# A smaller DMA scratch, paired probability buffers for the last query tiles, and another place in memory for the raw operands of the gate/up stage

## The chip, the core and the metric

The kernel runs on one core of one Trainium2 chip. The metric is the device time of one execution in microseconds (us), median of the runs. PE is the matrix engine (PEld its weight load), DVE the vector engine, ACT the scalar engine, POOL the GpSimd engine, SP the engine that issues most DMAs (SPq is its queue). SBUF is the on-chip memory of 128 partitions; every address below is a byte offset within one partition, taken from the sizes of the program's tiles.

## The reference, cut to what matters

One decoder layer over 1024 positions of width 1024, in float32:

```python
h = h + rms_norm(mixer(rms_norm(h, norm_mix_pre)), norm_mix_post)
h = h + rms_norm(swiglu(rms_norm(h, norm_ffn_pre)), norm_ffn_post)
# mixer: 8 attention heads (2 groups of 4) with three softmax branches (compressed blocks,
#   selected blocks, a window of 512), mixed by gates, beside 8 chunked spatial-gating groups,
#   all through one output projection w_out
# swiglu(h) = (silu(h @ w_gate) * (h @ w_up)) @ w_down, inner width 2816
```

## The kernel before

A float32 product is made of three float32r matmuls (`mm3`, L182 to L185): each operand is split into a rounded part (`hi`, a cast on ACT, L167) and a remainder (`lo`, a subtraction on DVE or POOL, L173), and hi*hi, hi*lo and lo*hi are summed in PSUM.

The stages follow each other: norm and input projections, compressed keys and values, attention, gate/up, down projection. A planner orders the instructions of each engine before the run by times of its own; each engine then works its list strictly in that order. `tc.high_priority(n)` moves a block ahead in the planner's choice, otherwise program order decides between instructions that are ready.

**Memory.** Tiles live in pools, and pools are stacked from two ends. The left stack begins behind the DMA scratch (16,384 bytes, at address 0) and grows up; the right one begins at 229,344 and grows down. When a pool is closed its bytes are handed to the next pool opened there, and a new tile waits until every tile that held any of its bytes has been read for the last time (`reuse_waits="tile"`). So the stack order decides what a load or a split has to wait for.

**Attention** (L639 to L762) goes over the eight query tiles of 128 rows from tile 7 down to tile 0, and in each over four pairs of heads (`g`, `pr`). For each head, PE makes logits in a PSUM bank `a` (L673, L674; two banks, handed out strictly in turn), DVE adds the bias and writes them to the head's probability buffer `L` with its running minimum (L678, L682), ACT takes exponentials in place (L721), POOL multiplies by gate over sum in place (L732), PE transposes the blocks (L745), ACT and DVE split them (`ph`, `pl`), and PE multiplies with the values `vt` and `vch` (L752, L754). There are six `L` buffers of 6,912 bytes, taken in turn; tiles 7 to 0 use 64 heads in all. The queries of a pair are loaded by `load_q` (L567) two pairs ahead and split on POOL. In pair 1 of a tile `output_proj` of the tile before is issued (L595, matmuls into banks `w`), in pair 3 its `pre_ffn` (L625), which writes the normalised, transposed rows to DRAM (`h2_scr[1]` for tiles 7 to 4, `h2_scr[0]` for tiles 3 to 0, L637). For tile 0 both come behind the loop (L763).

**Gate/up** is one level of a Strassen-like scheme with seven products. Seven regions of 16,384 bytes on the right hold the activation operands (`bps`, L783). `raw1` is half 1 of the rows (loaded from `h2_scr[1]`, L802), `b12` and `b22` are its split halves; `praw` is the raw weights of the first column block (L813), `pop` and four `op` tiles their splits. `plain_pass(1, b12, b22)` (L874) is the first matmul work of the stage, 96 matmuls of 512 columns, and needs nothing of tiles 3 to 0. Then `raw0` is loaded (half 0, needs tile 0's `h2_scr` rows), split to `b11`, `b21`, `plain_pass(0, ...)` runs, and sums and splits of `raw0` and `raw1` give `t1` to `t4`. Only then is `raw0`'s memory handed to the sums `s` of the weights (L939), which the products 6, 7, 5 and 3 of the next block need; the products 1, 2 and 4 do not.

The addresses that matter, before:

| region | address | region | address |
|---|---|---|---|
| L0 .. L5 | 126,464 .. 167,936 | r1t4 (`raw1`, later `t4`) | 212,480 .. 228,864 |
| o, q (queries) | 167,936 .. 179,712 | b22 | 196,096 .. 212,480 |
| bias tables B, C, MW | 181,248 .. 194,560 | b12t3 (`b12`, later `t3`) | 179,712 .. 196,096 |
| `vt` | 194,560 .. 210,944 | t1 (`pop`, later `t1`) | 163,328 .. 179,712 |
| `kt0`, `kt1` (keys) | 210,944 .. 227,840 | t2 | 146,944 .. 163,328 |
| `vch` | 227,840 .. 228,864 | b11 (`praw`, later `b11`) | 130,560 .. 146,944 |

Of the kernel before, what the change touches and what calls it, by code (L numbers as in the profile page):

```python
# [9 lines left out]
F32 = mybir.dt.float32  # L10
F32R = mybir.dt.float32r
# [6 lines left out]
P = 128  # L18
S = 1024
# [51 lines left out]
def trunk_kernel(ctx, tc, x, rel_bias, norm_mix_pre, norm_mix_post, norm_ffn_pre, norm_ffn_post, w_in,  # L71
# [3 lines left out]
    nc = tc.nc  # L75
# [37 lines left out]
    def turn(key, tags):  # L113
        n = turns.get(key, 0)
        turns[key] = n + 1
        return bank(tags[n % len(tags)])
# [435 lines left out]
    at = {}  # L552
    for nm in ("pt", "mix", "late", "L", "o", "q"):
        if nm == "L":
            at[nm] = Ring("at_L", 6, "left")
            at[nm].pools.reverse()
            g_at.append(at[nm])
            continue
        g_, at[nm] = pool("at_" + nm, 1, "left")
        g_at.append(g_)  # L560
# [6 lines left out]
    def load_q(i, g, pr):  # L567
        qr = at["q"].tile([P, 2, P], F32, name="qr", bufs=2)
        h0 = g * R + 2 * pr
        for dup in range(2):  # L570
            nc.sync.dma_start(out=qr[64 * dup:64 * dup + 64],
                              in_=q_scr[h0:h0 + 2, :, i * P:(i + 1) * P].rearrange("h d t -> d h t"))
        qt = at["q"].tile([P, 2, 2, P], F32R, name="qt", bufs=4)
        split(qt[:, 0], qt[:, 1], qr, "pool", "pool")
        return qt
# [3 lines left out]
    qts = {}  # L579
    for key in order[:2]:  # L580
        qts[key] = load_q(*key)
# [7 lines left out]
    HP0, HP, HP2, HO, HF, HQ, HS, HV = 400, 100, 150, 100, 400, 300, 600, 200  # L589
# [48 lines left out]

    for ti, i in enumerate(TILES):  # L639
# [5 lines left out]
        for g in range(G):  # L645
            for pr in range(2):
# [15 lines left out]
                with tc.high_priority(HP0 if at_ < 4 else HP if i >= 4 else HP2):  # L662
                    for hh in range(2):
                        r = pr * 2 + hh
                        h = g * R + r
                        L = at["L"].tile([P, 64 + S + 640], F32, "L")
# [96 lines left out]
    pre_ffn(TILES[-1], *output_proj(TILES[-1]))  # L763
# [10 lines left out]
    def acc_bank():  # L774
        if fbanks is None:
            return turn("plain", "awap")
        return fbanks.tile([P, 512], F32, name="fb")
# [5 lines left out]
    for tag in ("r1t4", "b22", "b12t3", "t1", "t2", "b11", "b21"):  # L783
        g_, bps[tag] = pool("ffn_" + tag, 1, "right")
        g_b.append(g_)

    def btile(tag, dtype=F32R):
        return bps[tag].tile([P, 2, HK, 512], dtype, name="b_" + tag, tag=tag)
# [9 lines left out]
    def h2_load(dst, half):  # L798
        for a in range(2):
            for kq in range(2):  # L800
                k = a * HK + 2 * kq
                nc.sync.dma_start(out=dst[:, a, 2 * kq:2 * kq + 2], in_=h2_scr[half][:, k:k + 2, :])  # L802

    raw1 = btile("r1t4", F32)
    h2_load(raw1, 1)
# [5 lines left out]
    def load_w(r, m, fp, a):  # L811
        c0 = m * DFF + fp * 256
        nc.sync.dma_start(out=r, in_=wgu[:, a * HK:(a + 1) * HK, c0:c0 + 256])  # L813
# [47 lines left out]
    pop = bps["t1"].tile([P, 4, 2, HK, P], F32R, name="plain_op", tag="t1")  # L861
    plain = {}
    for m in range(2):
        for a in range(2):
            load_w(praw[:, m, a], m, 0, a)
    for j in range(2):
        for m in range(2):
            plain[m, j] = [operand(praw[:, m, a, :, j * P:(j + 1) * P], pop[:, 2 * m + a] if j == 0 else None)
                           for a in range(2)]
    for a, dst in enumerate((b12, b22)):  # L870
        for k in range(HK):
            bsplit(dst, raw1[:, a, k], k)
# [39 lines left out]
    t1 = btile("t1")  # L912
    for k in range(HK):
        bsplit(t1, raw0[:, 0, k], k, PF_T1)
# [4 lines left out]
    t4_ = btile("r1t4")  # L919
# [287 lines left out]
```

## Time and profile before

| what | value |
|---|---|
| median of 3 runs | 1248.43 us (1248.29 to 1248.55) |
| the profiled execution | 1249.3 us, of which the span of instructions is 1247.6 us |
| PE busy | 1204.6 us (97%) |
| DVE, ACT, POOL busy | 917.0, 569.7, 379.5 us |
| mean granted clock of PE | 0.994 |

The busy time is summed over stages with different limits, so a stage is read from its own stretch of the timeline: which engine is idle there, and what ended its wait. [...]

### The profile page before, as it was taken

How to read it: one execution, taken by the hardware profiler on the slowest of the kernel's cores; microseconds unless marked ns; L12 is line 12 of the kernel's file. 1: busy time of each engine (PE TensorE's matmuls, PEld its weight loads, DVE VectorE, ACT ScalarE, POOL GpSimd, SP SyncE). 2: the span in 40 equal slices, each digit the busy share in tenths (PEclk: the TensorE clock that was granted, in tenths of full speed). 3: DMA queues.
4: the chain of work that ended last, by engine and by line, in shares of the span. 5: the costliest groups of instructions: out<-in, count | busy, mean ns of one | idle time of the engine just before them, and what ended most of it. 6: DMA issues, size and time to landing. Idle time of an engine off the chain costs nothing. (4 is left out here: it accounts for less than half of the span.)

```text
span 1247.6 us, 18252 instructions
## 1 busy us (share of the span) xinstructions
PE 1204.6 (97%) x6074; PEld 1006.7 (81%) x6074; DVE 917.0 (74%) x2075; ACT 569.7 (46%) x1266; POOL 379.5 (30%) x453
## 2 busy tenths in 40 slices
PE   6999999889999999999899999999999999999997
PEld 5888878868888888887687888888888888888886
DVE  5646247658898899876589877877787647588996
ACT  4423022247777778876544332333332324544452
POOL 3315112164444455642151222201222201132341
PEclk9999999999999999999899999999999999999999
DMA  7213453331111222215604233223233189333335
GB/s 255 85 68 87 133 185 116 106 100 46 43 48 47 61 64 71 66 56 159 226 37 145 96 122 127 94 91 107 89 127 126 53 281 365 120 110 85 93 119 202
DMA packets 106229, 143.86 MB, mean 115 GB/s; under 512 B 8120, under 2 KB 64792, under 8 KB 106136
## 3 DMA queue, kind: packets, MB, share of 16 engines
q1 hardware_dynamic: 99552, 133.43, 32.7%
q10 hardware_dynamic: 4280, 5.08, 1.2%
q0 software_dynamic: 2304, 4.20, 1.2%
q8 instruction: 48, 0.79, 0.3%
q14 instruction: 45, 0.37, 0.1%
HBM read 103.60 MB, written 40.71 MB: 116 GB/s over the span
## 5 line engine op out<-in xcount | busy, mean ns | idle before, releaser
L960 DVE TENSOR_TENSOR cc<-fb,cc 128x512 f32<-128x512 f32 x140 | 94.3, 687 | 56.8 <-PE fb L185 55.9
L732 POOL TENSOR_SCALAR L<-L,wts 128x64 f32<-128x64 f32 (+8 forms) x192 | 107.1, 580 | 88.3 <-DVE wts L727 56.6
L721 ACT ACTIVATE L<-L,mm 128x64 f32<-128x64 f32 (+8 forms) x192 | 116.2, 607 | 23.8 <-DVE mm L678 23.0
L849 POOL TENSOR_TENSOR cc<-sil 128x512 f32<-128x512 f32 x22 | 35.2, 1601 | 288.0 <-issue 225.5
L173 DVE TENSOR_TENSOR pl<-ps_t,ph 128x512 fp32r<-128x512 f32 (+2 forms) x168 | 102.9, 619 | 20.9 <-ACT ph L167 20.4
L167 ACT CAST ph<-ps_t 128x512 fp32r<-128x512 f32 (+2 forms) x168 | 87.1, 531 | 43.7 <-PE ps_t L745 39.2
L167 ACT CAST op<-s 128x512 fp32r<-128x512 f32 x80 | 49.4, 620 | 121.1 <-PE fb L185 107.2
L184 PE MATMUL fb<-wdo,hido 128*128 128x512 f32 x264 | 102.7, 389 | 0.0
L183 PE MATMUL fb<-wdo,hido 128*128 128x512 f32 x264 | 101.9, 389 | 0.0
L185 PE MATMUL fb<-wdo,hido 128*128 128x512 f32 x264 | 100.4, 389 | 0.0
L184 PE MATMUL fb<-b_b,op 128*128 128x512 f32 x256 | 99.6, 389 | 0.0
L185 PE MATMUL fb<-b_b,op 128*128 128x512 f32 x256 | 99.4, 389 | 0.0
L183 PE MATMUL fb<-b_b,op 128*128 128x512 f32 x256 | 99.3, 389 | 0.0
L745 PE MATMUL ps_t<-ident,L 128*128 128x128 f32 (+1 forms) x592 | 93.9, 274 | 3.6 <-POOL L L732 2.6
L173 DVE TENSOR_TENSOR hido<-hidr,hido 128x512 fp32r<-128x512 f32 x77 | 60.8, 801 | 26.7 <-ACT hido L167 26.6
L673 PE MATMUL ps_a<-kt,qt 128*128 128x448 f32 (+4 forms) x208 | 75.0, 364 | 4.7 <-DVE L L682 2.0
L745 PEld LDWEIGHTS ps_t<-ident,L 128*128 128x128 f32 (+1 forms) x592 | 68.2, 137 | 12.4 <-POOL L L732 4.6
L167 ACT CAST hido<-hidr 128x512 fp32r<-128x512 f32 x77 | 47.3, 619 | 65.8 <-PE fb L185 26.7
L1039 POOL TENSOR_TENSOR tt<-wdr 128x512 f32<-128x512 f32 x22 | 36.1, 1644 | 134.7 <-DVE wdo L173 79.9
L167 ACT CAST op<-wraw 128x512 fp32r<-128x512 f32 x60 | 37.0, 622 | 84.6 <-PE fb L185 73.1
L173 DVE TENSOR_TENSOR op<-s,op 128x512 fp32r<-128x512 f32 x80 | 63.7, 801 | 15.1 <-ACT op L167 14.2
L752 PE MATMUL ps_p<-ph,vt 128*128 128x256 f32 x264 | 73.3, 295 | 0.2 <-ACT ph L167 0.2
(357 smaller groups left out, 3458.5 us busy)
## 6 DMA issues: line engine op xcount, KB each, us to landing
wraw<-in_w_gate_up_dram SPq DMA_DIRECT2D x40, 512.0 KB, 3.5
hidr<-hid_scr SPq DMA_DIRECT2D x77, 256.0 KB, 2.7
hid_scr<-sil SPq DMA_DIRECT2D x44, 256.0 KB, 2.0
wdr<-in_w_down_dram SPq DMA_DIRECT2D x44, 256.0 KB, 5.3
hid_scr<-cc SPq DMA_DIRECT2D x33, 256.0 KB, 2.0
xt<-in_x_dram SPq DMA_DIRECT2D x16, 512.0 KB, 4.9
raw<-in_w_in_dram SPq DMA_DIRECT2D x16, 512.0 KB, 3.5
gm_scr<-gmt SPq DMA_DIRECT2D x16, 256.0 KB, 2.7
```

The costliest lines, as they stand in the source:

```text
L167: nc.scalar.copy(hi, src)
L173: e.tensor_tensor(lo, src, fl(hi), op=ALU.subtract)
L183: nc.tensor.matmul(ps, sh, mh, start=first, stop=False)
L184: nc.tensor.matmul(ps, sh, ml, start=False, stop=False)
L185: nc.tensor.matmul(ps, sl, mh, start=False, stop=last)
L673: nc.tensor.matmul(ps[:, :w], qt[:, 0, hh, :], kt_[g][:, c0:c0 + w], start=True, stop=False)
L721: nc.scalar.activation(L[:, c0:c1], L[:, c0:c1], AF.Exp, bias=mm[:, col:col + 1], scale=-1.0, accum_out=sums[:, hh, br:br + 1])
L732: nc.gpsimd.tensor_scalar(pts[hh][:, c0:c1], pts[hh][:, c0:c1], wts[:, hh, br:br + 1], 1.0, op0=ALU.mult, op1=ALU.mult)
L745: nc.tensor.transpose(ps[:kk, (bi * 2 + hh) * P:(bi * 2 + hh + 1) * P], pts[hh][:, c0:c0 + kk], ident)
L752: nc.tensor.matmul(pv[:, :256], v, ph[:kk, bi * 256:(bi + 1) * 256], start=(gi == 0 and bi == 0), stop=False)
L960: nc.vector.tensor_tensor(dst, ps, y_, op=ALU.add)
L1039: eng.tensor_tensor(dst, x_, y_, op=op)
```

## The change

Five parts:

1. The DMA scratch at the bottom of SBUF shrinks from 16,384 to 2,048 bytes. The whole left stack moves down by 14,336 bytes; the right one stays.
2. The attention pools are stacked in the order pt, mix, late, o, q, L, so that the six L buffers lie on top. Tiles 7 to 4 use six of them, tile 3 uses five (L0 to L4), and tiles 2 to 0 use L0 to L2, each holding both heads of a pair. The first two pairs' queries are loaded into L5 and split into L4.
3. On the right, `raw1` shares a region with `t1` instead of `t4`, and `pop` with `t4` instead of `t1`; the order of the regions changes.
4. `output_proj` and `pre_ffn` of tile 0 get priority (HE = 100), loads and splits of the first gate/up operands are interleaved in another order, `t3` is split before `t1`.
5. The accumulators of the two plain passes come from banks a, a, a, p instead of a, w, a, p (only the first pass uses them).

The addresses after, from the same sizes:

| region | address | region | address |
|---|---|---|---|
| o, q | 112,128 .. 123,904 | t4 (`pop`, later `t4`) | 212,480 .. 228,864 |
| L0, L1, L2 | 123,904 .. 144,640 | b22 | 196,096 .. 212,480 |
| L3, L4 | 144,640 .. 158,464 | b12t3 | 179,712 .. 196,096 |
| L5 | 158,464 .. 165,376 | r1t1 (`raw1`, later `t1`) | 163,328 .. 179,712 |
| nothing | 165,376 .. 181,248 | b11 (`praw`, later `b11`) | 146,944 .. 163,328 |
| `vt`, keys, `vch`, bias tables | as before | t2 | 130,560 .. 146,944 |

```diff
-    for nm in ("pt", "mix", "late", "L", "o", "q"):
+    for nm in ("pt", "mix", "late", "o", "q", "L"):
         if nm == "L":
             at[nm] = Ring("at_L", 6, "left")
-            at[nm].pools.reverse()
...
-    for key in order[:2]:
-        qts[key] = load_q(*key)
+    q0r = at["L"].pools[5][1].tile([P, 2, 2, P], F32, name="L")
+    q0t = at["L"].pools[4][1].tile([P, 2, 2, 2, P], F32R, name="L")
+    for n, key in enumerate(order[:2]):
+        qts[key] = load_q(*key, (q0r[:, n], q0t[:, n]))
...
+    def lring(i):
+        n = lturn["n"]
+        lturn["n"] += 1
+        ps_ = at["L"].pools
+        if n < 4:
+            return ps_[3 - n][1]
+        return ps_[5 - (n - 4) % 6][1] if i > 3 else ps_[4 - n % 5][1]
+
+    def lpair(n):
+        return at["L"].pools[2 - n % 3][1]
...
+                    if i <= 2:
+                        Lp = lpair(at_).tile([P, 2, 832], F32, name="L")
...
-                        L = at["L"].tile([P, 64 + S + 640], F32, "L")
+                        L = Lp[:, hh] if i <= 2 else lring(i).tile([P, 64 + S + 640], F32, name="L")
...
-    pre_ffn(TILES[-1], *output_proj(TILES[-1]))
+    with tc.high_priority(HE):
+        pre_ffn(TILES[-1], *output_proj(TILES[-1]))
...
-            return turn("plain", "awap")
+            return turn("plain", "aaap")
...
-    for tag in ("r1t4", "b22", "b12t3", "t1", "t2", "b11", "b21"):
+    for tag in ("t4", "b22", "b12t3", "r1t1", "b11", "t2", "b21"):
...
-    raw1 = btile("r1t4", F32)
-    h2_load(raw1, 1)
+    raw1 = btile("r1t1", F32)
...
-    pop = bps["t1"].tile([P, 4, 2, HK, P], F32R, name="plain_op", tag="t1")
+    pop = bps["t4"].tile([P, 4, 2, HK, P], F32R, name="plain_op", tag="t4")
...
-    for m in range(2):
-        for a in range(2):
-            load_w(praw[:, m, a], m, 0, a)
-    for j in range(2):
-        for m in range(2):
-            plain[m, j] = [operand(praw[:, m, a, :, j * P:(j + 1) * P], pop[:, 2 * m + a] if j == 0 else None)
-                           for a in range(2)]
-    for a, dst in enumerate((b12, b22)):
-        for k in range(HK):
-            bsplit(dst, raw1[:, a, k], k)
+    for a in range(2):
+        h2_load(raw1, 1, a)
+        load_w(praw[:, 0, a], 0, 0, a)
+    for a in range(2):
+        load_w(praw[:, 1, a], 1, 0, a)
+    for a, dst in enumerate((b12, b22)):
+        plain_op(0, 0, a)
+        for k in range(HK):
+            bsplit(dst, raw1[:, a, k], k)
+    for a in range(2):
+        plain_op(1, 0, a)
+    for m in range(2):
+        for a in range(2):
+            plain_op(m, 1, a)
...
-    t1 = btile("t1")
-    for k in range(HK):
-        bsplit(t1, raw0[:, 0, k], k, PF_T1)
...
     sub_all(raw0[:, 1], raw0[:, 1], raw1[:, 1])
-    t4_ = btile("r1t4")
+    t1 = btile("r1t1")
+    for k in range(HK):
+        bsplit(t1, raw0[:, 0, k], k, PF_T1)
+    t4_ = btile("t4")
...
-    nc = _bacc.Bacc("TRN2", target_bir_lowering=False, num_devices=1)
+    nc = _bacc.Bacc("TRN2", target_bir_lowering=False, num_devices=1, dynamic_dma_scratch_size=2048)
```

## Rows read from the trace of the kernel before

**Rows 1.** The page: busy time of PE, and the queue of POOL's DMAs.
```profile
PE 1204.6 (97%) x6074; PEld 1006.7 (81%) x6074; DVE 917.0 (74%) x2075; ACT 569.7 (46%) x1266; POOL 379.5 (30%) x453
...
q0 software_dynamic: 2304, 4.20, 1.2%
```

**Rows 2.** Windows: length, busy us of five engines, clock, DMA share, GB/s.
```profile
400.00:500.00 100.00, 98.53 (x644) 85.50 (x643) 89.60 (x349) 77.48 (x208) 48.61 (x85) 1.00 0.22 65
500.00:550.00 50.00, 47.86 (x307) 40.70 (x305) 41.80 (x186) 42.03 (x137) 30.59 (x64) 1.00 0.20 61
...
594.00:604.00 10.00, 5.45 (x13) 4.26 (x14) 7.68 (x14) 8.93 (x19) 0.55 (x1) 0.66 0.91 342
...
650.00:660.00 10.00, 7.64 (x31) 5.10 (x30) 8.53 (x7) 2.93 (x6) 8.03 (x6) 1.00 0.41 131
660.00:1200.00 540.00, 540.00 (x2384) 447.27 (x2383) 411.21 (x583) 200.60 (x349) 105.99 (x66) 1.00 0.39 130
```

**Rows 3.** Timeline of PE, 590 to 604: start, length, ..., [idle before <-releaser].
```profile
590.46 0.28 PE L754 MATMUL ps_p<-pl,vt 128*128 128x256 f32 x1
592.19 0.50 PE L183 MATMUL ps_w<-whi,mixh 128*128 128x512 f32 x1 [1.46 <-ACT mixh L167]
...
593.23 0.62 PE L185 MATMUL ps_w<-whi,mixl 128*128 128x512 f32 x2
598.55 0.80 PE L183 MATMUL ps_a<-b_b12t,plain_op 128*128 128x512 f32 x1 [4.71 <-ACT b_b12t L167]
...
603.83 0.40 PE L183 MATMUL ps_a<-b_b12t,plain_op 128*128 128x512 f32 x1
```

**Rows 4.** Timeline of SP's DMA queue, 588 to 597.
```profile
588.75 0.53 SPq L813 DMA_DIRECT2D plain_raw<-in_w_gate_up_dram  x1
589.37 2.59 SPq L802 DMA_DIRECT2D b_r1t<-h_scr  x4
592.15 4.85 SPq L813 DMA_DIRECT2D plain_raw<-in_w_gate_up_dram  x3
```

**Rows 5.** Timeline of ACT and DVE, 595 to 606.
```profile
595.05 0.62 ACT L167 CAST plain_op<-plain_raw 128x512 fp32r<-128x512 f32 x1 [2.91 <-DMA plain_raw<-in_w_gate_up_dram]
...
597.89 1.13 ACT L167 CAST b_b12t<-b_r1t 128x512 fp32r<-128x512 f32 x2
...
603.48 2.49 DVE L173 TENSOR_TENSOR b_b<-b_r1t,b_b 128x512 fp32r<-128x512 f32 x4
```

**Rows 6.** Timeline of ACT, 620 to 624: the first casts of raw0.
```profile
620.81 2.33 ACT L167 CAST b_b<-raw 128x512 fp32r<-128x512 f32 x4 [1.22 <-DMA raw<-h_scr]
```

**Rows 7.** Timeline of POOL and DVE, 634 to 652: splits, first weight sum.
```profile
634.33 6.34 POOL L173 TENSOR_TENSOR b_b12t<-b_r1t,b_b12t 128x512 fp32r<-128x512 f32 x2 [24.28 <-ACT b_b12t L167]
...
648.85 2.56 POOL L173 TENSOR_TENSOR b_r1t<-raw,b_r1t 128x512 fp32r<-128x512 f32 x2 [1.83 <-issue]
...
651.43 0.69 DVE L939 TENSOR_TENSOR s<-wraw 128x512 f32<-128x512 f32 x1 [1.83 <-POOL b_r1t L173]
```

**Rows 8.** Timeline of DVE, PE and POOL at two changes of query tile.
```profile
453.30 0.22 DVE L678 CUSTOM_DVE_ANT_0 L<-ps_a,C 128x64 f32<-128x64 f32 x1
...
461.92 0.60 PE L745 MATMUL ps_t<-ident,L 128*128 128x128 f32 x4
...
489.56 0.22 DVE L678 CUSTOM_DVE_ANT_0 L<-ps_a,C 128x64 f32<-128x64 f32 x1
...
491.69 3.27 POOL L732 TENSOR_SCALAR L<-L,wts 128x64 f32<-128x64 f32 x6 [2.77 <-DVE wts L727]
```

**Rows 9.** Timeline of PE and POOL where attention begins.
```profile
240.83 0.28 PE L185 MATMUL ps_p<-w2s,chidT 128*128 128x64 f32 x1
...
242.59 0.40 POOL L171 TENSOR_SCALAR qt<-qr 128x256 fp32r<-128x256 f32 x1 [7.82 <-DMA qr<-q_scr]
```

**Rows 10.** The tile gmh: the DMAs that POOL issues.
```profile
L601 POOL DMA_DIRECT2D gmh<-gm_scr x16: 535/574/777, 250.5 to 560.7; - x16
...
DMA to landing us min/median/max: 2.8/3.1/4.4
```

More of the change, by code (lines that the diff above doesn't have):

```diff
@@ L565, in load_bc, with load_q @@
         bcast_load(bc["post"], norm_mix_post[0])
-    def load_q(i, g, pr):
-        qr = at["q"].tile([P, 2, P], F32, name="qr", bufs=2)
+    def load_q(i, g, pr, start=None):
+        if start is None:
+            qr = at["q"].tile([P, 2, P], F32, name="qr", bufs=2)
+            qt = at["q"].tile([P, 2, 2, P], F32R, name="qt", bufs=4)
+        else:
+            qr, qt = start
         h0 = g * R + 2 * pr
@@ L572, in load_q @@
                               in_=q_scr[h0:h0 + 2, :, i * P:(i + 1) * P].rearrange("h d t -> d h t"))
-        qt = at["q"].tile([P, 2, 2, P], F32R, name="qt", bufs=4)
         split(qt[:, 0], qt[:, 1], qr, "pool", "pool")
@@ L588, in trunk_kernel @@
     wout_args = {}
-    HP0, HP, HP2, HO, HF, HQ, HS, HV = 400, 100, 150, 100, 400, 300, 600, 200
+    HE, HP0, HP, HP2, HO, HF, HQ, HS, HV = 100, 400, 100, 150, 100, 400, 300, 600, 200
     PVB, OPB, OB = "p", "w", 1
@@ L637, in pre_ffn @@
             nc.sync.dma_start(out=h2_scr[i // 4][:, 4 * b:4 * b + 4, (i % 4) * P:(i % 4 + 1) * P], in_=tl)
+    lturn = {"n": 0}
+    def lring(i):
[7 more added lines that the diff above has]
+        return at["L"].pools[2 - n % 3][1]
     for ti, i in enumerate(TILES):
@@ L796, in bsplit, with h2_load @@
         split(dst[:, 0, k], dst[:, 1, k], src, "act", "dve" if k < pool_from else "pool")
-    def h2_load(dst, half):
-        for a in range(2):
+    def h2_load(dst, half, *parts):
+        for a in parts or range(2):
             for kq in range(2):
@@ L860, in trunk_kernel, with plain_op @@
     praw = bps["b11"].tile([P, 2, 2, HK, 256], F32, name="plain_raw", tag="b11")
-    pop = bps["t1"].tile([P, 4, 2, HK, P], F32R, name="plain_op", tag="t1")
+    pop = bps["t4"].tile([P, 4, 2, HK, P], F32R, name="plain_op", tag="t4")
     plain = {}
+    def plain_op(m, j, a):
+        plain.setdefault((m, j), [None, None])[a] = operand(praw[:, m, a, :, j * P:(j + 1) * P],
+                                                            pop[:, 2 * m + a] if j == 0 else None)
+    for a in range(2):
[9 more added lines that the diff above has]
+        plain_op(1, 0, a)
     for m in range(2):
         for a in range(2):
-            load_w(praw[:, m, a], m, 0, a)
-    for j in range(2):
-        for m in range(2):
-            plain[m, j] = [operand(praw[:, m, a, :, j * P:(j + 1) * P], pop[:, 2 * m + a] if j == 0 else None)
-                           for a in range(2)]
-    for a, dst in enumerate((b12, b22)):
-        for k in range(HK):
-            bsplit(dst, raw1[:, a, k], k)
+            plain_op(m, 1, a)
     def plain_pass(half, blo, bhi):
```

## The prediction

> **What bounds the kernel now.** I read the page first, then the windows stage by stage, then the timelines of the stretches where PE is idle. PE is busy for 97% of the span [rows 1], and from 660 to 1200 us it never stops: 2384 matmuls in 540 us, 0.2265 us each [rows 2]. No part of the change lies there, so it can only win or lose in the other stretches, and the largest loss near it is the seam between attention and gate/up. The timeline of PE shows the seam. The last product with the values starts at 590.46; then PE waits 1.46 us for tile 0's last mixing operand, ends tile 0's output projection at 593.85 (593.23 + 0.62), and waits again, 4.71 us, until 598.55, when the first gate/up matmul starts [rows 3]. [...] A second, smaller stop follows at 650 to 660, where PE is busy for 7.64 of 10 us [rows 2].
>
> What ends the 4.71 us is a cast of `b12`, and that cast waits for data. SP issues the load of `raw1` at 589.37 and most of the raw weights from 592.15 [rows 4]; the DMA engines are 0.91 busy from 594 to 604 [rows 2]; the first split of the weights starts at 595.05 behind a wait for its load, that of `b12` at 597.89 [rows 5]. Both loads were late because of where they lie: `raw1` over the keys and `vch`, which the very last pair still reads, and `praw` over L0 to L2.
>
> **Part by part.** *The raw loads.* After the change `raw1` (163,328 up) shares bytes only with L5, and `praw` (146,944 up) with L3 to L5. Tile 3 is the last to use L3 and L4, tile 4 the last with L5, so both loads can go out from the start of tile 2 at about 490 [rows 8], a hundred microseconds early. The 4 MB are hidden under tiles 2 to 0, where the DMA share is 0.20 [rows 2]; without that cover they would cost what they cost now. What is late next? `pop` lies on the keys and `vch`, `b12` and `b22` on the bias tables, `vt` and a key: all wait for the last values product at 590.46 or shortly before it. So the splits start at about 591. Sixteen of them are needed for the first pass, at DVE's pace of 0.62 us (four in 2.49 us) [rows 5], while each k-step of PE takes 3 x 0.2265 = 0.68 us. PE can go from tile 0's projection (593.85) straight into gate/up instead of at 598.55: 4.7 us less. I leave the 1.46 us before as they are; a gain of all of it is the bound. If PE does not stand long, the twelve slow matmuls run at 0.2265: 12 x (0.44 - 0.2265) = 2.6 us less. Against that, DVE also has tile 0's norm and residual between the splits, some five 512-wide operations, 5 x 0.62 = 3.1 us, with priority HE. PE can use up the splits made before them, so I charge half, +1.5 us; the bounds are 0 and 4.5 us (all of it, and half of the clock loss again).
>
> *`raw0` and tile 0's chain.* The second pass needs `raw0`, cast from 620.81 [rows 6]. The first pass is 96 matmuls, 96 x 0.2265 = 21.7 us; from 593.85 with 1.5 us of holes it ends at 617.1. Today's first split of `raw0` would be whole at 620.81 + 0.62 (cast) + 0.62 (remainder) = 622.0, which is 4.9 us too late. The chain before it is tile 0's norm, residual, second norm, transposes, a write and a read of DRAM, and it shares DVE and ACT with the sixteen splits (16 x 0.62 = 9.9 us of DVE). HE moves exactly this chain ahead of them, so I take it as early enough: 0, bound +4.9 us.
>
> *`t1`, `t4` and the weight sums.* Before, `t4` waited for `raw1`'s memory, its POOL splits ended at 651.41 (648.85 + 2.56), and only then the first sum started, at 651.43 [rows 7]; PE lost 10 - 7.64 = 2.36 us [rows 2]. After, `t4` waits for `pop`, which the second pass ends with, and `t1` for `raw1`; products 1, 2 and 4 (3 x 12 x 0.2265 = 8.2 us) still cover the sums, and DVE's work there starts earlier with `raw0`. I take 1.5 us of the 2.36, bounds 0 and 2.36. POOL's splits took 3.17 us each when DVE ran beside them and 1.28 when it hardly did [rows 7]. [...]
>
> *Buffers of tiles 3 to 0.* The depth is the same or nearly so (three pairs; five heads in tile 3), but the turns collide. The last head of tile 4 is number 31 and lies in L2 (5 - 27 % 6), and the first of tile 3, number 32, in L2 too (4 - 32 % 5). The first pair of tile 2 (number 20) takes L0, the buffer of tile 3's last head (39). Each first pair thus waits until the pair before it is transposed. Now head 32 is written from 453.30, while head 31's transposes run until about 462 (one group of four starts at 461.92); tile 2's first head is written from 489.56, while POOL scales tile 3's last pair from 491.69 to 494.96 [rows 8]. So two first pairs start 7 to 9 us later. Behind them stand all later logits, since the two banks `a` are handed out in turn. PE has other work: the output projection of the tile before, 48 matmuls or 10.9 us, and DVE is 90% and 84% busy around there [rows 2], so it catches up. I charge 1.5 us in all; bounds 0 and 10 us.
>
> *Entry to attention.* The first queries now land in L5, over the compression's `chidT` (159,360 up), last read at 240.83; before, POOL split them at 242.59 [rows 9]. A load after 241.1 comes at best 1 us later, with value projections to fill PE. +0.5 us, bounds -1.5 and +2. *Banks a, a, a, p, the order of loads, the scratch itself:* 0. Banks `w` are still tile 0's, so no wait is lost or added before two accumulators are full; POOL issues 16 small DMAs of 0.57 us in the whole kernel, two for each tile [rows 10].
>
> The sum: -4.7 - 2.6 + 1.5 + 0 - 1.5 + 1.5 + 0.5 = -5.3 us. The profiled execution took 1249.3 us, so 1244.0; it is 0.9 above the median of the runs, which becomes 1248.4 - 5.3 = 1243.1.
>
> **Rivals.** *Tile 0's chain is the new bound.* If `raw0` comes when it comes now, PE stands 4.9 us after the first pass: 1248.0, no change. For it: DVE and ACT still have all the splits to do beside it. Against: HE, and 9.9 us of splits that it may pass. 0.12.
> *The splits are the new bound.* The first splits can't start before 591, and if PE stands for 4.5 us while they are made, the seam is only moved: -5.3 + 3.0, and without the gain at 650 to 660, 1246.9; no change. For it: `b12` and `b22` still wait for `vt`. Against: 0.62 is below 0.68. 0.08.
> *The colliding turns make it slower.* At each of the two tile changes PE runs dry for half of the 9 to 11 us of delay, 10 us together: -5.3 - 1.5 + 10 = +3.2, 1251.6. It decides from 6.8 us. For it: PE has 0.98 of 1 in 400 to 500 and no spare pair. Against: the projections wait there as filler. 0.12.
> *The small scratch stalls POOL.* If the second of two DMAs had to wait for the first, POOL's scaling behind it would be 3.1 us late (the median landing) in each of eight tiles [rows 10]; if half of that reached PE, -5.3 + 12.4 = +7.1 us, 1255.5. Against: 2304 packets in all [rows 1], for 16 DMAs on 16 engines 9 each, and two such DMAs a tile. [...] 0.04.
>
> **How the numbers follow.** The forecast has 0.64. What a measurement here tells from no change is about 0.2%, 2.5 us. Faster by more: the forecast, 0.64. Within: the first two rivals, 0.20. Slower: the last two, 0.16. The bounds of the terms reach down to 1238 (all of 1.46 and 2.36, no charge at the tile changes); upward I take the slower rival's edge, 1251, which leaves about 0.2 outside.
>
> **What would show it.** `raw1` and `praw` issued before 560; the first gate/up matmul within 1 us of tile 0's projection, at full clock; no wait of PE for a cast of `b_b` at the second pass; PE's idle time in 650 to 660 below 1 us. The turns show as late writes to L at the two tile changes and idle PE near 465 and 500. I am wrong if attention ends several us later, or if a wait for splits as long as 4.7 us stands in place of the old one.

## The result, and the profile after

The kernel after takes 1265.12 us (median of 4, 1264.83 to 1267.01) against 1248.49 of before on the same chip: 16.6 us slower, ratio 1.0129 (95% interval 1.0106 to 1.0151). Forecast were 1243.1 us and, at the upper end of the range, 1251. Its profiled execution took 1265.1 us with a span of 1263.4.

The windows of the kernel after, with the columns of [rows 2]:

```profile
400.00:500.00 100.00, 96.45 (x615) 81.88 (x614) 83.25 (x315) 74.05 (x193) 47.43 (x80) 1.00 0.17 54
500.00:550.00 50.00, 47.80 (x295) 39.39 (x294) 44.10 (x188) 39.94 (x128) 30.06 (x59) 1.00 0.52 167
...
650.00:660.00 10.00, 10.00 (x46) 8.29 (x45) 8.26 (x11) 4.43 (x8) 10.00 (x4) 1.00 0.07 26
660.00:1200.00 540.00, 537.63 (x2371) 444.51 (x2371) 407.26 (x570) 196.60 (x341) 115.50 (x73) 1.00 0.38 130
```

PE issues 615 matmuls from 400 to 500 us where it issued 644, and 295 against 307 in the 50 us behind: attention is already late there. The stop of PE at 650 to 660 [rows 2] has only moved on, beyond 660: PE is idle for 2.37 us there (540 - 537.63) against 2.36 before. The seam, in the timeline of PE after:

```profile
603.08 0.28 PE L773 MATMUL ps_p<-pl,vt 128*128 128x256 f32 x1
604.39 0.73 PE L183 MATMUL ps_a<-b_b12t,plain_op 128*128 128x512 f32 x2 [1.03 <-ACT b_b12t L167]
606.37 0.80 PE L184 MATMUL ps_a<-b_b12t,plain_op 128*128 128x512 f32 x1 [1.24 <-DVE b_b12t L173]
...
611.66 0.50 PE L184 MATMUL ps_a<-b_b12t,plain_op 128*128 128x512 f32 x1
...
614.31 0.39 PE L183 MATMUL ps_w<-whi,mixh 128*128 128x512 f32 x1
...
615.44 0.62 PE L185 MATMUL ps_w<-whi,mixl 128*128 128x512 f32 x2
...
637.64 1.22 PE L183 MATMUL fb<-b_b,plain_op 128*128 128x512 f32 x2 [4.83 <-ACT b_b L167]
```

Against [rows 3] the reader sees three things. The last product with the values comes 12.6 us later. The first gate/up matmul follows it after 1.31 us instead of 8.09: this is what the change was forecast to win. Not all of it is won, because 1.66 us of the 8.09 were the last six matmuls of tile 0's output projection [rows 3, 592.19 to 593.85], which have only moved behind; PE's idle time at the seam falls from 6.17 us (1.46 + 4.71) to 2.27 us (1.03 + 1.24). And that projection, which ended ahead of gate/up before, now ends inside it, at 616, and some 22 us later PE's wait of 4.83 us for the first cast of `raw0` ends, a wait that was not there before. What stood in ACT's and DVE's queues ahead of the operand that the projection needed (timeline of ACT and DVE after):

```profile
601.04 2.18 ACT L167 CAST plain_op<-plain_raw 128x512 fp32r<-128x512 f32 x4
603.45 0.37 ACT L775 COPY otmp<-ps_p 64x256 f32<-64x256 f32 x1 [0.24 <-PE ps_p L773]
603.73 2.18 ACT L167 CAST b_b12t<-b_r1t 128x512 fp32r<-128x512 f32 x4
605.81 2.17 ACT L167 CAST b_b<-b_r1t 128x512 fp32r<-128x512 f32 x4
607.89 0.29 ACT L167 CAST mixh<-os 128x128 fp32r<-128x128 f32 x1
...
602.61 2.48 DVE L173 TENSOR_TENSOR plain_op<-plain_raw,plain_op 128x512 fp32r<-128x512 f32 x4
605.01 0.58 DVE L778 TENSOR_TENSOR os<-ps_p,otmp 64x128 f32<-64x128 f32 x2
610.45 0.28 DVE L173 TENSOR_TENSOR mixl<-os,mixh 128x128 fp32r<-128x128 f32 x1
```

`mixh` and `mixl` stand last, behind eight casts and eight remainders of `b12` and `b22`. PE's own list has the projection late as well: its six matmuls start at 614.31, behind 25 gate/up matmuls and 3.6 us after `mixl` is ready (610.73). Everything that follows from them is late, to the first cast of `raw0`:

```profile
636.97 2.39 ACT L167 CAST b_b<-raw 128x512 fp32r<-128x512 f32 x4 [6.25 <-DMA raw<-h_scr]
```

16.2 us later than [rows 6]. The raw loads themselves went out as forecast, 77 to 90 us before they did (DMA queue of SP, after):

```profile
502.01 2.04 SPq L832 DMA_DIRECT2D plain_raw<-in_w_gate_up_dram  x4
...
512.22 2.76 SPq L822 DMA_DIRECT2D b_r1t<-h_scr  x4
```

The change from tile 3 to tile 2, timeline of POOL and DVE after: POOL scales tile 3's last pair, DVE then writes tile 2's first head, POOL scales that pair.

```profile
501.61 3.39 POOL L751 TENSOR_SCALAR L<-L,wts 128x64 f32<-128x64 f32 x6 [1.52 <-ACT mixh L167]
...
510.05 0.22 DVE L697 CUSTOM_DVE_ANT_0 L<-ps_a,C 128x64 f32<-128x64 f32 x1 [0.87 <-PE ps_t L764]
...
516.48 2.84 POOL L751 TENSOR_SCALAR L<-L,wts 128x64 f32<-128x64 f32 x6 [2.38 <-DVE wts L746]
```

From one scaling to the next it takes 14.87 us; DVE's write is released by a transposition of the pair before, which by the rule of the turns reads the same buffer, L0. Before, the write came 2.1 us ahead of the last pair's scaling [rows 8].

The entry to attention, timeline of SP's queue and POOL, in the kernel before:

```profile
259.87 0.81 SPq L130 DMA_DIRECT2D wo_raw<-in_w_out_dram  x2
...
264.73 1.05 POOL L161 TENSOR_SCALAR whi<-wo_raw 128x1024 fp32r<-128x1024 f32 x1 [3.34 <-DMA wo_raw<-in_w_out_dram]
...
268.21 4.34 POOL L732 TENSOR_SCALAR L<-L,wts 128x64 f32<-128x64 f32 x6
```

The same with PE, after:

```profile
249.93 11.68 SPq L574 DMA_DIRECT2D qr<-q_scr  x12
261.65 12.39 SPq L130 DMA_DIRECT2D wo_raw<-in_w_out_dram  x3
...
270.22 1.04 POOL L161 TENSOR_SCALAR whi<-wo_raw 128x1024 fp32r<-128x1024 f32 x1 [8.98 <-DMA wo_raw<-in_w_out_dram]
...
273.67 4.34 POOL L751 TENSOR_SCALAR L<-L,wts 128x64 f32<-128x64 f32 x6
...
274.04 0.71 PE L764 MATMUL ps_t<-ident,L 128*64 128x128 f32 x2 [6.13 <-POOL L L751]
```

In both kernels POOL has the split of the first output weight queued ahead of the first pair's scaling. Before, PE waits 2.0 us for that scaling; after, the weight comes 5.5 us later (270.22 against 264.73) and PE waits 6.13 us. The loads of output weights leave SP's queue, behind twelve loads of queries, only 1.8 us later than before (261.65 against 259.87); the larger part is their way from issue to landing, 8.4 to 9.0 us against 4.8 to 6.2.

The first microseconds differ too. Timeline of SP's queue and of ACT's, first in the kernel before, then after:

```profile
4.86 5.38 SPq L130 DMA_DIRECT2D xt<-in_x_dram  x2
...
167.19 0.32 ACTq L415 DMA_DIRECT2D pos_nat<-in_cmp_pos_k_dram  x1
```

```profile
0.80 0.42 ACTq L415 DMA_DIRECT2D pos_nat<-in_cmp_pos_k_dram  x1
...
7.01 3.30 SPq L130 DMA_DIRECT2D xt<-in_x_dram  x2
```

Four small loads of the compression, which went out at 167 to 173 us, now go out at 0.8 to 6.3 us, and the second pair of loads of x leaves SP 2.15 us later.

**A table of lateness.** The profiled executions reach attention between 0.4 us earlier and 3.4 us later than that of before, so the runs below are compared from one event on: POOL's fill of the bias table (L508), at 233.89 us before and 235.01 after. The table gives starts, in us later (+) or earlier than in the kernel before; all columns but the first are counted from that fill. "First pair" is the sum (L778) of tile 7's first pair, "tile 3" and "tile 2" that of their last pairs, "last PV" the last product with the values, "raw0" its first cast, "967" the matmul of the main loop that stood at 967.0 us before, "end" the last matmul. Each row is one execution: the profiled one took 2.5 us more than its kernel's median in e1 and 3.1 more in e11, 2.7 less in e7 and 2.1 less in e10, so a difference below some 3 us at the end of two rows is not an effect by itself.

| run | fill | first pair | tile 3 | tile 2 | last PV | first gate/up | raw0 | 967 | end |
|---|---|---|---|---|---|---|---|---|---|
| after | +1.1 | +4.3 | +3.0 | +9.8 | +11.5 | +4.7 | +15.0 | +14.7 | +14.7 |
| e1_turns | +3.4 | +5.1 | +3.7 | +4.2 | +5.9 | -0.9 | +9.6 | +9.2 | +9.2 |
| e2_entry | +0.5 | -1.4 | -1.8 | +5.3 | +6.8 | +0.4 | +10.4 | +10.9 | +10.9 |
| e3_chain | +2.4 | +4.6 | +3.3 | +10.1 | +12.0 | +5.4 | +8.7 | +7.5 | +7.5 |
| e4_scratch | +2.6 | +0.1 | -0.7 | -1.1 | +0.4 | -2.3 | +1.5 | +0.8 | +0.8 |
| e5_three | +0.6 | -1.6 | -2.0 | +1.3 | +3.2 | -3.4 | +1.3 | +0.7 | +0.7 |
| e6_pool | +0.5 | -1.2 | -1.6 | +1.7 | +3.5 | -3.3 | +2.3 | +0.4 | +0.4 |
| e7_swap | +0.9 | -2.6 | -3.3 | 0.0 | +2.0 | -4.6 | -1.3 | -2.5 | -2.6 |
| e8_late | +1.1 | -1.3 | -1.7 | +1.6 | +2.4 | +6.0 | +3.2 | +6.8 | +14.1 |
| e9_anchor | +0.2 | -2.2 | -4.4 | -4.6 | -2.7 | -8.6 | -2.9 | -4.7 | -4.8 |
| e10_hold | +0.3 | -2.5 | -4.7 | -4.9 | -4.1 | -10.8 | -2.9 | -3.5 | -3.5 |
| e11_scratch_anchor | +0.4 | +0.1 | 0.0 | 0.0 | 0.0 | -0.2 | +0.1 | +2.9 | +2.9 |
| e12_torder | +0.3 | -1.2 | -3.4 | -3.6 | -2.8 | -9.5 | -0.8 | -1.4 | +6.4 |
| e13_after_anchor | -0.4 | +4.8 | +3.6 | +10.4 | +12.1 | +5.3 | +15.4 | +15.0 | +15.0 |
| e14_late2 | +0.6 | -2.1 | -4.3 | -4.5 | -3.7 | +0.2 | -2.4 | +1.1 | +8.4 |

The row of after holds the story: 4.3 us lost at the entry, 6.8 between the ends of tiles 3 and 2, 6.8 won at the seam (+11.5 to +4.7, with the 1.66 us of projection that only moved), 10.3 lost again up to `raw0`.

### The profile page after: what moved, and what is told of

It is laid out like the page before. It is cut to its first block, busy times and chain, and to the rows that moved or that the text cites. A ratio compares the mean times of both kernels' runs of the same rounds, so it can differ in the third digit from the quotient of the medians.

```text
span 1263.4 us, 18216 instructions
## 1 busy us (share of the span) xinstructions
PE 1209.8 (96%) x6074; PEld 1007.8 (80%) x6074; DVE 917.4 (73%) x2075; ACT 569.4 (45%) x1266; POOL 384.9 (30%) x453
## 5 line engine op out<-in xcount | busy, mean ns | idle before, releaser
L751 POOL TENSOR_SCALAR L<-L,wts 128x64 f32<-128x64 f32 (+8 forms) x192 | 109.7, 593 | 83.5 <-DVE wts L746 46.9
L773 PE MATMUL ps_p<-pl,vt 128*128 128x256 f32 x264 | 72.8, 299 | 1.6 <-DVE pl L173 1.5
```

What stands on the lines that cost most here:

```text
L751: nc.gpsimd.tensor_scalar(pts[hh][:, c0:c1], pts[hh][:, c0:c1], wts[:, hh, br:br + 1], 1.0, op0=ALU.mult, op1=ALU.mult)
L773: nc.tensor.matmul(pv[:, :256], v, pl[:kk, bi * 256:(bi + 1) * 256], start=False, stop=last)
```

## Experiments

**e1_turns: the buffers of L in an order without collision.**

```diff
-        return ps_[5 - (n - 4) % 6][1] if i > 3 else ps_[4 - n % 5][1]
+        return ps_[5 - (n - 4) % 6][1] if i > 3 else ps_[(33 - n) % 5][1]
 ...
-        return at["L"].pools[2 - n % 3][1]
+        return at["L"].pools[2 - (n + 1) % 3][1]
```

> The kernel after, with the turns of L ordered so that each tile change takes the buffer that was freed longest ago: tile 3's heads start at L1 instead of L2, tile 2's pairs at L2 instead of L0. Theory A (four separate delays; the colliding turns are one): in the kernel after the pairs run 4.1 us late at the end of tile 3 and 10.9 us late at the end of tile 2; the 6.8 us between them are the collision, so the time falls by about 7 us, 1258, and the first head of tile 2 is written within 2 us of the last of tile 3. Theory B (the early raw loads delay the tile change: the DMA engines are 0.95 busy from 510 to 520 us): the turns matter little, the lateness of 10 us after tile 2 stays, 1264 to 1266.

1259.55 us, ratio 1.0082 (1.0061 to 1.0102). In the table the loss between tiles 3 and 2 falls from 6.8 to 0.5 us, the end from +14.7 to +9.2. POOL's scalings at this tile change:

```profile
503.34 3.29 POOL L751 TENSOR_SCALAR L<-L,wts 128x64 f32<-128x64 f32 x6 [4.71 <-DVE wts L746]
...
511.17 2.86 POOL L751 TENSOR_SCALAR L<-L,wts 128x64 f32<-128x64 f32 x6 [3.35 <-DVE wts L746]
```

7.83 us apart instead of 14.87 (7.69 in the kernel before), with the early raw loads still under this stretch. The collision cost 5.5 us by the table, 5.6 by the medians; theory B (the early loads' traffic) falls.

**e2_entry: the first two loads of output weights on ACT's queue.**

```diff
+    def wload(src, raw=None, leng=None, q=None):
 ...
-        dma(view(raw), src)
+        (q or nc.sync).dma_start(out=view(raw), in_=src)
 ...
-            wo[k] = wload(w_out_v[:, k, :], raw, WOE)
+            wo[k] = wload(w_out_v[:, k, :], raw, WOE, nc.scalar if len(wo) < 7 else None)
```

> The kernel after, with the first two loads of the output weights on ACT's queue instead of SP's, where they stand behind twelve loads of queries. Theory A: the lateness of the first pair (5.4 us, of which 4 to 5 us never come back) is the wait for these weights on POOL, which scales the first pair only after it has split them; the time falls by 4 to 5 us, 1260.5, and PE's longest wait for POOL's scaling near 275 us falls from 6.1 to about 2 us. Theory B: the first logits, 1.7 us late because the queries of the first pairs lie over the last tiles of the compression, are the delay that stays: the gain is 3 us at most, 1262 to 1265.

1261.81 us, ratio 1.0095 (1.0076 to 1.0115); the first pair comes at -1.4 instead of +4.3, the end at +10.9: 3.8 us. The planner now also places the first scaling ahead of the weights' split on POOL, and it orders the whole of attention anew:

```profile
261.58 0.90 ACTq L158 DMA_DIRECT2D wo_raw<-in_w_out_dram  x2
...
265.93 4.37 POOL L751 TENSOR_SCALAR L<-L,wts 128x64 f32<-128x64 f32 x6 [5.01 <-DVE wts L746]
270.27 2.06 POOL L161 TENSOR_SCALAR whi<-wo_raw 128x1024 fp32r<-128x1024 f32 x2
```

PE's longest wait for POOL's scaling in that stretch, 6.1 us in after, is 0.3 here. Theory A in what POOL waits for, but not in the reason that it gave: on ACT's queue the loads leave at the same time as on SP's (261.58 against 261.65), and POOL's first split starts at the same time (270.27 against 270.22). The place on SP's queue cost next to nothing; what the edit took away is the place of the weights' split ahead of the scaling in POOL's list. By the medians it gives 3.3 us.

**e3_chain: the last mixing operand of the last pair on POOL.**

```diff
-                    split(mixh[:, g * 2 + pr, :], mixl[:, g * 2 + pr, :], os_)
+                    me = ("pool", "pool") if at_ == len(order) - 1 else ("act", "dve")
+                    split(mixh[:, g * 2 + pr, :], mixl[:, g * 2 + pr, :], os_, *me)
```

> The kernel after, with the last mixing operand of the last pair split on POOL, which is idle there, instead of on ACT and DVE behind sixteen splits of the gate/up stage. Theory A: tile 0's chain is late only by that place in the queues; the projection ends some 6 us earlier, the first cast of raw0 comes at about 631 instead of 637, PE's 4.8 us of waiting before the second pass and the slow clock behind it go: 6 to 8 us less, 1258. Theory B: the norm and the transposes of the chain still share DVE and ACT with the splits, and the load of raw0 comes as late as before: 1263 to 1265.

1258.07 us, ratio 1.0065 (1.0044 to 1.0086). POOL has the operand ready at 608.9, the first cast of `raw0` comes at 631.87:

```profile
607.22 0.79 POOL L171 TENSOR_SCALAR mixh<-os 128x128 fp32r<-128x128 f32 x1 [11.36 <-DVE os L778]
608.09 0.77 POOL L173 TENSOR_TENSOR mixl<-os,mixh 128x128 fp32r<-128x128 f32 x1
...
631.87 2.38 ACT L167 CAST b_b<-raw 128x512 fp32r<-128x512 f32 x4 [1.80 <-DMA raw<-h_scr]
```

The wait of 4.83 us is gone, while e1 and e2, which leave this split alone, still have it (4.94 and 4.8 us). The end moves from +14.7 to +7.5: 7.2 us (7.1 by the medians), theory A. With the operand on POOL the planner also puts the projection's first matmul third among those of gate/up, so the run shows the worth of both places together.

**e4_scratch: before, with `dynamic_dma_scratch_size=2048` alone.**

> The kernel before, with nothing but the dynamic DMA scratch of 2 KB. Theory A: the scratch alone changes nothing, 1248.4 within 0.2%, and the queue of POOL's DMAs looks as in the kernel before (median landing 3.1 us). Theory B (the small scratch makes the second of two DMAs wait for the first): POOL's scaling behind it is late by some 3 us in each tile, 1251 to 1256, and it is part of the 16.6 us.

1250.84 us, ratio 1.0009 (0.9999 to 1.0019); the queue of POOL's DMAs has a median landing of 3.1 us as before. The rival "the small scratch stalls POOL" falls. What the scratch does change are addresses: all tiles of the left stack lie 14 KB lower, the four small loads no longer wait for memory, and they go out at 0.8 to 6.1 us here too. The planner's order of attention is another one as well.

**e5_three: the edits of e1, e2 and e3 together.**

> The kernel after with all three edits: turns, weights on ACT's queue, last operand on POOL. Theory A (three separate delays that add up): counted from the last fill of the bias tables, the kernel after ends 14.7 us later than the kernel before; the three runs of one edit each took 5.5, 3.8 and 7.2 us off; all three give 14.7 - 16.5 = 1.8 us earlier than before: 1245.5 to 1248. Theory B (they overlap: what one gives back, another wait takes): at least 4 us more than that, 1251 or above.

1250.62 us, ratio 1.0018 (1.0006 to 1.0030): some 14 us of the 16.6 are accounted for by three places, but it takes 2.6 to 5 us more than theory A gave, just short of theory B. By the table 3.3 us are lost between the ends of tiles 3 and 2 (-2.0 to +1.3), where e1 with the same turns lost 0.5, and the seam is entered later than the edits promised: the last product with the values is at +3.2 though tile 2 ended at +1.3.

**e6_pool and e7_swap: two more edits on e5.** e6 puts the remainders of the second half of the plain weights on POOL (`leng="pool"` for j = 1). e7 swaps `q0r` and `q0t` between L5 and L4.

> As e5, and the remainders of the second half of the plain weights on POOL instead of DVE. Theory A: these splits, made ready early by the early loads, stand on DVE ahead of the last pair's remainders; without them the last product with the values comes 1 us earlier, and DVE has 2.5 us less to do in the seam: 1 to 2 us less than e5. Theory B (POOL and DVE hold each other up, and the last operand waits behind them on POOL): 0 to 3 us more than e5.

1251.16 us, 1.0018 (1.0009 to 1.0027): no difference from e5; theory A's gain of 1 to 2 us is not there.

> As e5, and the first two pairs' raw queries in L4, over a tile that is free earlier, with their split in L5. The order of instructions on all engines is that of e5. Theory A (the entry's loss was the wait for the output weights): the first logits come 1 to 2 us earlier, and the time is that of e5 within 1 us, because value projections fill PE there. Theory B (the entry is paced by the first queries): 1.5 us or more less than e5.

1250.41 us, 1.0016 (1.0004 to 1.0027): no difference that its runs show, though the first pair of its profiled execution is 1.0 us earlier. Theory A, the entry is not paced by the first queries.

**e8_late: e5 with the placement undone.**

```diff
-    for tag in ("t4", "b22", "b12t3", "r1t1", "b11", "t2", "b21"):
+    for tag in ("t4", "r1t1", "b12t3", "b22", "t2", "b11", "b21"):
```

> As e5, with the raw operands placed on memory that is read to the end of attention again (raw1 on the bias tables' side, the plain weights over L1 to L3), so that their loads can't go early: the placement of the change taken back by itself. Theory A: the early loads are worth what the seam shows, some 5 us (the first gate/up matmul 1.3 us behind the last product with the values, against 8.1 before): 1251 to 1254. Theory B (the early loads give back what they win, since their splits crowd the last pair): within 2 us of e5.

1263.61 us, ratio 1.0123 (1.0107 to 1.0139), 13 us over e5. PE waits at the seam as it did before, and longer:

```profile
605.63 1.22 PE L183 MATMUL ps_a<-b_b12t,plain_op 128*128 128x512 f32 x2 [8.24 <-ACT b_b12t L167]
```

The table splits the 13 us: 6.1 up to 967 us (+0.7 to +6.8), and 7.3 behind it, in the down projection, where PE has waits of 2.3, 1.4 and 1.1 us that e5 has not. So neither theory's number holds for the whole; where the 7.3 us come from is read below, behind e14.

**e9_anchor and e11_scratch_anchor: the four small loads held back.** e9 is e7 with this, e11 is e4 with it.

```diff
+        nc.vector.tensor_copy(pn[:, 0:1], state["qs"][0:16, 0:1])
         nc.scalar.dma_start(out=pn, in_=pos[0]...
 ...
+        nc.vector.tensor_copy(w2r[:, 0, 0:1], state["qs"][:, 0:1])
         nc.scalar.dma_start(out=w2r, in_=w2[0]...
```

> As e7 (three edits and the swapped queries), and the four small loads of the compression (positions and second weights) made to wait for the last queries, by a copy of one column of theirs into each destination. Theory A: with the 2 KB scratch all tiles lie 14 KB lower, these four loads no longer wait for memory, go out at 0.8 to 6 us instead of at 167 to 173, and slow the first loads; all nine programs with the small scratch reach the fill of the bias tables 0.5 to 3.4 us later than the kernel before. Held back, the first eight loads on SP's queue go out as in the kernel before (the last pair of them at 4.9 instead of 7.0 us), and the time falls by 1 to 2 us against e7: 1248 to 1249. Theory B (the first 20 us differ by chance from run to run): no change, 1250.4.

1244.12 us, ratio 0.9963 (0.9950 to 0.9976): faster than both kernels. The loads of x leave SP at 4.90 us again, and the fill comes at +0.2. But 6.3 us against e7 are more than the start can give. The two profiled executions (1247.70 and 1244.75 us) show 2.95 of them: 0.7 at the fill, and 2.2 behind it, where tile 2 ends 4.6 us earlier than in e7: the 3.3 us that e5 and e7 lose between the ends of tiles 3 and 2 are not lost here (-4.4 to -4.6). Behind the held loads the planner makes another order of the whole attention; that this order is what wins them was not tested by itself.

> The kernel before with the 2 KB scratch (as e4) and the same four loads held back. Theory A (addresses are all that the scratch changes): the 0.1% that e4 was slower goes, 1.0000 within 0.001. Theory B (the small scratch itself slows the queues): as e4, 1.0009 or more.

1249.49 us, ratio 1.0008 (0.9996 to 1.0020): inconclusive by time. By the table attention repeats the kernel before to 0.2 us, up to `raw0`; PE has the same order of instructions in both. The 2.9 us behind that come from the clock. A window of the kernel before, and two of e11:

```profile
660.00:670.00 10.00, 10.00 (x46) 8.26 (x45) 9.05 (x16) 4.68 (x9) 0.00 (x0) 1.00 0.51 159
```

```profile
650.00:660.00 10.00, 7.68 (x31) 5.12 (x29) 8.13 (x8) 2.45 (x5) 8.51 (x6) 0.96 0.38 127
660.00:670.00 10.00, 9.97 (x31) 7.97 (x32) 9.22 (x16) 5.16 (x10) 0.00 (x0) 0.70 0.53 163
```

The same idle PE at 650 to 660 (7.64 us busy [rows 2], and 7.68; three waits of 0.73, 0.30 and 1.33 us in one, of 0.73, 0.30 and 1.32 in the other) is followed by 46 matmuls at clock 1.00 in one execution and by 31 at 0.70 in the other.

**e10_hold: e9 with twelve operand splits held back** until the last pair's sum (a copy of one column of `os` into each operand ahead of its split, on POOL).

> As e9, and twelve operand splits that the early loads made ready before the end of attention (the second half of the plain weights, two of the first half, the first pairs of the main loop) held back until the last pair's output is there. Theory A: these splits, in DVE's and ACT's queues between the last pair's, make the last products with the values 2 to 3 us late (3.1 us later than before in e5, of which 0.9 were there at the pair ahead of it); without them PE's waits for the remainders (0.9 us) and before the first gate/up matmul (1.0 us) shrink and the time falls by 2 to 3 us against e9: about 1246. Theory B: the splits are only moved, to the time in which tile 0's chain needs DVE and ACT; raw0 comes later and the time is that of e9 or up to 2 us more.

1248.12 us, ratio 0.9993 (0.9984 to 1.0003): 4 us more than e9, of which its profiled execution, 2 us faster than its median, shows 1.3. Theory A falls; theory B gave at most 2 us and a later `raw0`, so it holds only in that nothing is won. Attention ends 1.4 us earlier (-2.7 to -4.1) and the first gate/up matmul comes 2.2 us earlier, but `raw0` comes at the same time, so PE now waits 3.62 us for it, 0.2 in e9:

```profile
588.05 0.50 PE L183 MATMUL ps_a<-b_b12t,plain_op 128*128 128x512 f32 x1 [1.12 <-ACT b_b12t L167]
...
618.83 1.22 PE L183 MATMUL fb<-b_b,plain_op 128*128 128x512 f32 x2 [3.62 <-ACT b_b L167]
```

**e12_torder: e10 with t1 and t4 in the order and sharing of before.**

> As e10, with t1 and t4 in the order and with the sharing of before: t1 is written over the plain operands and ahead of t3, t4 over raw1 and last. Theory A (my term of -1.5 us: the new order lets PE off the stall at the first sums): 1 to 2 us more than e10. Theory B (the stall hangs on DVE's and POOL's work, which is the same in either order; the kernel after shows the wait at 2.4 us against 1.6 before): within 1 us of e10.

1255.80 us, ratio 1.0050 (1.0037 to 1.0062). It is not what it seems: from `raw0` to 967 us both kernels gain the same 0.6 us (-0.8 to -1.4, and -2.9 to -3.5 in e10), and 7.8 us are lost behind that (-1.4 to +6.4), in the down projection:

```profile
1032.93 0.73 PE L183 MATMUL fb<-wdo,hido 128*128 128x512 f32 x1 [4.04 <-ACT hido L167]
1040.02 1.20 PE L185 MATMUL fb<-wdo,hido 128*128 128x512 f32 x4 [1.58 <-DVE hido L173]
```

For the stage in question the order is worth nothing: theory B.

**e13_after_anchor: the kernel after with the held loads alone; e14_late2: e9 with the placement undone as in e8.**

> The kernel after, with nothing but the four small loads held back as in e9. Theory A: they cost the kernel after what the start shows, about 1 us until the fill of the bias tables (235.0 against 233.9): 1263.5 to 1264.5, and all later delays stay. Theory B: what e9 won over e7 (6 us, of which the start accounts for 1 to 1.5) came from the other order that the planner makes behind the held loads: 1259 to 1261 here too.

1263.85 us, ratio 1.0114 (1.0094 to 1.0135), 1.3 us less than after; the fill moves by 1.5 us, the rest of the row is that of after. Theory A: the small loads are some 1.3 us of the 16.6. The times alone do not show it, since the two intervals overlap and e4 and e11 have the same ratio; the fill does, at +0.5 to +3.4 in the nine programs that let these loads go early and at -0.4 to +0.6 in the six that hold them.

> As e9, with the raw operands back on memory that is read to the end of attention, as e8 was to e5; e8 was 13 us slower than e5, but 7.3 of them arose after 1200 us, in the down projection, where the planner had made another order. Theory A: the early loads are worth 6 us up to the end of gate/up, and the rest of e8 was that other order: 1249 to 1251.5 if the order after gate/up is that of e9. Theory B: late loads cost the whole 13 us: 1256 or more.

1256.66 us, ratio 1.0057 (1.0042 to 1.0072): up to 967 us the early loads are worth 5.8 us (-4.7 to +1.1), as theory A said; 7.3 us more are lost in the down projection, as in e8 and e12, so the condition of theory A (the same order behind) did not hold.

**Where the 7.3 to 7.8 us in the down projection come from.** The traces and the addresses answer it. In every program with the small scratch the buffers `wdo`, for the split weights of the down projection, lie at 144,896 to 169,472. Behind 163,328 this is the region r1t1, which holds `t1` last, in e5, e9 and e10; the region of `b22` in e8 and e14; and r1t1 with `t4` in it in e12. The last reads of that region by PE, and the casts into `wdo` on ACT, in e9, e14 and e12:

```profile
1016.91 0.39 PE L185 MATMUL fb<-b_r1t,op 128*128 128x512 f32 x1
1017.33 2.71 ACT L167 CAST wdo<-wdr 128x512 fp32r<-128x512 f32 x5 [4.82 <-PE fb L185]
```

```profile
1028.64 0.39 PE L185 MATMUL fb<-b_b,op 128*128 128x512 f32 x1
1029.06 2.71 ACT L167 CAST wdo<-wdr 128x512 fp32r<-128x512 f32 x5 [10.26 <-PE fb L185]
```

```profile
1028.50 0.39 PE L185 MATMUL fb<-b_r1t,op 128*128 128x512 f32 x1
1028.92 2.69 ACT L167 CAST wdo<-wdr 128x512 fp32r<-128x512 f32 x5 [12.97 <-DMA hid_scr<-sil]
```

(The view's `b_b` covers `b11`, `b21` and `b22`; the line shown is the last that reads `b22`.) In each the casts start 0.03 us after that last read has ended; in e12 the view names a DMA out of `sil` as the releaser, and the time fits PE's read there too. The last products of gate/up take 2.72 us each (12 matmuls) and read `t1`, `b21`, `b22`, `t4` in this order: with `b22` under `wdo` the casts wait two products longer than with `t1`, with `t4` three. So a placement that was changed for the start of gate/up also decided when the down projection could start. No run tests this by itself.

## Why the prediction was wrong

The gain forecast at the seam is there in part; three costs that it put at 0, +1.5 and +0.5 measure 7.2, 5.5 and 3.8 us when each is taken off alone, and some 1.3 us come from the start. The largest of them, tile 0's chain at 0, is the step that failed. The three make 16.5 us one by one but some 14 together (e5), so what the rest of the change wins or loses can't be read off as the remainder.

- *-4.7 us, the first gate/up matmul directly behind tile 0: right in mechanism.* Raw loads at 502 and 512 us; last product with the values to gate/up 1.31 instead of 8.09 us, of which 1.66 us is projection that moved behind, so PE is idle for 3.9 us less. By itself, with the collisions, the entry and the start mended, the placement is worth 5.8 us (e9 against e14, up to 967 us).
- *-2.6 us, the slow clock: wrong.* PE still stands 1.03 and 1.24 us at the seam, and the eleven matmuls from 606.97 to 611.66 take 0.43 us each, at a granted clock of 0.50 (1.00 is full speed); that of 600 to 610 is 0.75. The term's twelve are those from 598.55 to 603.83 in the kernel before [rows 3], (603.83 - 598.55) / 12 = 0.44 us each, with a clock of 0.66 in 594 to 604 [rows 2]. That a shorter stand of PE keeps the clock was the author's estimate, and no run shows it: here 2.27 us of idle time instead of 6.17 did not.
- *+1.5 us, splits at DVE's pace: inside its bounds* of 0 to 4.5 (1.03 + 1.24 us), but by luck. The charge was for tile 0's norm between the splits; that norm came only behind them, at 616 to 621 us, and what PE waited for were the first cast and the first remainder of `b12`.
- *0 for tile 0's chain "thanks to HE": this step failed, 7.2 us (e3).* The prediction said that HE "moves exactly this chain ahead" of the splits. HE stands around the output projection and what follows; the split of `mixh` and `mixl`, on which the projection waits, is in the loop of attention. With HE = 0 the kernel has the same order of instructions on all five engines: HE does nothing. (This is read from the built programs, not from a run; with HE = 1000 the order changes, and `mixh` and `mixl` still stand behind the same sixteen instructions.) The early data made eight casts and eight remainders ready at the moment when this one pair of instructions was not yet ready, and the planner put them first. It is the rival "tile 0's chain is the new bound" (0.12), with a larger price than its 4.9 us, since the slow clock followed the new wait: the granted clock is 0.79 from 630 to 640 us and 0.87 from 640 to 650, and 1.00 in both in e3. That the new wait of 4.83 us is so near the rival's 4.9 is chance: the rival had `raw0` coming when it came before, and it came 16.2 us later.
- *-1.5 us, the stall at the first sums: wrong, 0.* PE's wait for DVE's operand there is 2.4 us in after against 1.6 before, and all its idle time at that stop 2.37 against 2.36; the order of t1 and t4 made no difference there (e12).
- *+1.5 us, the colliding turns: the size is wrong, 5.5 us (e1).* The place was right, and so was the wait of 7 us at the change to tile 2. At the change to tile 3 nothing is lost by that tile's end: +4.3 to +3.0 in the table from the first pair on, and +5.1 to +3.7 in e1, which has no collision there. At tile 2 the delay stayed to the end. The prediction gave DVE's busy share there (0.84) as room to catch up, and only a fifth of the delay was caught up.
- *+0.5 us, the entry: the mechanism is wrong, 3.8 us (e2).* Only the first pairs' queries were looked at, and e7 shows that they do not pace the entry. What cost time stands on POOL, where the split of the first output weight is queued ahead of the first pair's scaling: that weight came 5.5 us later, 1.8 of them at its issue (1.1 of these are the late start) and the rest on its way to landing. Why the landing took longer is open. To ask what each engine has queued ahead of the first pair's work would have found the place.
- *0 for the scratch: some 1.3 us (e13),* by none of the ways considered. The rival weighed against it, POOL's queue, is excluded by e4; the addresses alone, 14 KB lower, freed four loads to go out too early.

Two small sums of the prediction are off and change none of its chances: the terms of the second rival give 1247.6 and not 1246.9 (-5.3 + 3.0 + 1.5 = -0.8), and the terms named for the lower end give 1239.3; 1238 also takes the splits at 0.

The version that beats both is e9 (1244.12 us, 4.5 us under before): the change with its three faults and the start mended. What stays open: e9's gain over e7 is larger than the start explains and comes with another order of attention that the planner made; which instruction in it counts was not tried. That the 7.3 to 7.8 us in the down projection hang on which operand lies under `wdo` is read from times and addresses, and no run changed that alone. The banks a, a, a, p and the new order of the loads were not run by themselves.

## What to carry to other kernels

Here earlier loads (at 502 and 512 us instead of 589) made the splits behind them ready earlier, and the planner put sixteen of them into ACT's and DVE's lists ahead of the two instructions that the critical chain was about to need (DVE started `mixl` 2.3 us after `mixh` was ready, PE the projection 3.6 us after `mixl`). Name such an instruction before the run, and see that a priority encloses it and not only what follows, or give it to an idle engine, as e3 did (an enclosing priority was not run here). When buffers are handed out in turn and the rule of the turn changes, write down which buffer was freed last at each change and make the new turn start with the one freed first (worth 5.5 us here, e1). A change of a reserved size moves every address that is stacked on it (14 KB here), and with them which loads wait for memory (four went out at 0.8 to 6.1 us instead of 167 to 173, e4): compare the first loads of the two traces too. When two regions swap places, look at who gets their bytes last: here the next stage lost 7.3 to 7.8 us in the three programs (e8, e12, e14) where an operand that is read later lay under its first buffers, by their times and addresses.

## What was not expected of the hardware

The granted clock did not follow from the idle time alone: the same stop of PE (7.64 and 7.68 us busy in 10 us) left it at 1.00 in one execution (the kernel before) and took the next 10 us to 0.70 in the other (e11): 2.9 us between two executions that agree to 0.2 us for 390 us before. Longer stops at the same place kept 1.00 in e7 (16.89 of 20 us busy from 640 to 660) and e9 (17.11), against 17.64 before. And four small loads, 590 packets and 0.14 MB of the first 12 us, put the second pair of loads of x off by 2.15 us, though all queues together moved 3.27 MB in that time against 3.24 before. In the nine programs that let them go early this pair leaves at 6.93 to 8.02 us, in e9 to e12, which hold them back, at 4.90 to 5.62.
